# One exp per head with scale, bias and row sum, and one Silu per gate half, in the attention layer of a two-layer trunk

## The chip, the cores and the metric

The kernel runs on one core of one Trainium2 chip. TensorE (PE) multiplies matrices, VectorE (DVE), ScalarE (ACT) and GpSimd (POOL) do the work on elements, and SyncE (SP) issues most of the transfers. The metric is the device time of one execution in microseconds, here the median of several runs.

## The reference

Two layers over 2048 tokens of width 1024. The first is a gated linear recurrence (projection, short convolution, two gates, a scan over time, projection back). The second is an attention layer with 16 query heads of width 64 on 2 key and value heads, a window of 128 tokens, a position term and a learned sink per head. This is the part that matters here:

```python
def sliding_window_sink_attention(q, k, v, sinks):
    ...
    s = jnp.einsum('bnqkgd,bnskd->bnkgqs', qb, kb).astype(jnp.float32) * scale
    ...
    s = jnp.where(valid[None, :, None, None], s + alibi[None, None], -jnp.inf)
    sink = sinks.astype(jnp.float32).reshape(N_KV_HEADS, GROUP)[None, None, :, :, None, None]
    m = jnp.maximum(jnp.max(s, axis=-1, keepdims=True), sink)
    p = jnp.exp(s - m)
    denom = jnp.sum(p, axis=-1, keepdims=True) + jnp.exp(sink - m)
    p = (p / denom).astype(v.dtype)
    o = jnp.einsum('bnkgqs,bnskd->bnqkgd', p, vb)
    return o.reshape(bsz, seq, ATT_WIDTH)

def swa_layer(x, k, v, norm_g, w_in, q_norm_g, sinks, w_out):
    h = rmsnorm(x, norm_g)
    u = h @ w_in
    q, gate = u[..., :ATT_WIDTH], u[..., ATT_WIDTH:]
    q = rmsnorm(q.reshape(bsz, seq, N_Q_HEADS, HEAD_DIM), q_norm_g)
    o = sliding_window_sink_attention(q, k, v, sinks)
    y = o * jax.nn.silu(gate)
    return x + y @ w_out
```

## The kernel before

The kernel has three stages: layer A with channels on the partitions (until about 690 us), the projection out of A by blocks of 128 tokens (until about 955 us), and layer B, the attention layer. Every product of two float32 operands is made of three float16 products (high by high, high by low, low by high), so each value that TensorE is to read is first cut into two float16 parts: a cast and a subtraction.

Layer B works on 16 blocks of 128 tokens. `attend(b)` does the attention of block b; `between(b)` gives the other products that TensorE is to do meanwhile: the key, value and query projections of the next block (`project`), the projection out of the block before (`finish`) and the next block's gate (`project_gate`). `weave` takes so many of these after each step of `attend` as the numbers in `GAPS` say (in ns of TensorE's time). That sets the order in which the program is traced. The framework then orders the instructions of each engine: work that is ready by its own model of times goes first, and among ready work that which was traced first. On the chip each engine takes its instructions in that fixed order.

In `attend`, for each of eight pairs of heads, TensorE makes the scores against the block before and the own block (`o`, 3 buffers in PSUM). ScalarE copies one half to `s` (L961), VectorE puts in the other half by a mask (L962) and adds the position term with the row maximum (L967, one per head). After the fourth pair `soft(0)` works on heads 0 to 7, after the eighth `soft(1)` on heads 8 to 15: VectorE makes the shift `bi` for eight heads at once (L902 to L904), scales and shifts the scores of one head at a time (L906), ScalarE does one Exp over the eight heads (L907) and one for the sinks (L909). `cut` makes the two float16 parts of the weights (L925, L926), `turn` issues the transposing DMA `ppx<-ph` from SP's queue and two masked copies on GpSimd (L933), and `norms` makes the row sums (L913) and their reciprocals. `weigh` multiplies the transposed weights with the values into `po` (TensorE) and takes them out (L949, L950). `pT`, the target of the transpose, has one buffer, so the second half's transpose follows the first half's products. `scale_gate` multiplies the gate by the reciprocal sums on GpSimd (L920), and `gated` multiplies y by it, cuts it and transposes it.

`project` makes the norms of the keys (L810 to L817), their parts (L819), the values (L833 to L843; L842 waits for GpSimd's L841), and the query norms (L854 to L863, with a slow power on GpSimd at L860). `project_gate` makes the gate in two halves of 512 columns: a Sigmoid with a scale from a pointer out of PSUM (L883) and a product on VectorE (L884). The functions Sigmoid and Exp stand in different tables of ScalarE, and an instruction `ACT_TABLE_LOAD` stands ahead of each change from one to the other.

Of the kernel before, what the change touches and what calls it, by code (L numbers as in the profile page):

```python
# [17 lines left out]
AF = mybir.ActivationFunctionType  # L18
# [19 lines left out]
# other products woven in (columns / 2.4) after a block's pair of scores, before the first  # L38
# and the second half of its values; for the first block, the second, those between, the
# last but one, the last  # L40
# [13 lines left out]
def trunk(ctx, tc, x, wA, gw, par, gains, woA, wkv, wB, woB, vec, alib, out):  # L54
# [13 lines left out]
    # ---------------------------------------------------------------- constants  # L68
# [26 lines left out]
    def floor2(mx, n, keep):  # L95
        """[P, n] maxima -> keep [P, n]: each column's maximum over the partitions, rounded
        down to a power of two, on every partition"""
# [21 lines left out]
    # ------------------------------------------------ conv and decay parameters  # L119
# [14 lines left out]
    def decay():  # L134
        # softplus(-lam) = max(-lam, 0) + log1p(exp(-|lam|)), log1p(e) = 2 atanh(e / (2 + e))
# [27 lines left out]
    # ------------------------------------------------------------ shared pieces  # L163
# [3 lines left out]
    def absmax_rows(src, nk, gcol, dest):  # L167
        """largest |gain * w| per partition of src [P, nk, n] -> dest [P, 1]"""
        a = col("amx", nk)
        dve.tensor_reduce(a, src, AX.X, ALU.max, apply_absolute_value=True)  # L170
        dve.tensor_tensor(a, a, gabs[:, gcol : gcol + nk], ALU.mult)
        dve.tensor_reduce(dest, a, AX.X, ALU.max)
# [6 lines left out]
    def split_flat(src, scale, hi, lo):  # L179
        """hi + lo = src * scale in two f16 parts"""  # L180
# [3 lines left out]
    def rstd10(ss, eng):  # L184
        """2**10 / rms of rows of D from their sums of squares"""
# [8 lines left out]
    def normalize(xb, hi, lo, rs=pool):  # L194
        """hi + lo = rows of xb [P tok, D] over their rms, times 2**10"""
# [14 lines left out]
    def flip(src, dest):  # L210
        """dest[:, i, :] = the transpose of src[:, i * P : (i + 1) * P], two-byte types"""
        nc.sync.dma_start_transpose(dest, src)
# [13 lines left out]
    # ======================================================= layer A, channel-major  # L226
# [17 lines left out]
    def xparts():  # L244
        """two [P, D] f16 tiles"""
# [61 lines left out]
    def scales_x(g, W):  # L307
        # |conv(u) + b| <= sum|w| * 2**11 px + max|b|
# [43 lines left out]
    def proj_first(w):  # L352
        """the first chunk's three tiles, token block by token block"""
# [16 lines left out]
    def unit(g, c, W):  # L370
# [36 lines left out]
        def gate(w):  # L407
# [5 lines left out]
            # the fourth block, gathered, on the array's columns 0, 32 and 64  # L413
# [62 lines left out]
    # ---- the first weights and tokens  # L476
# [104 lines left out]
    # ============================================================== out-proj of A  # L581
# [40 lines left out]
    def bstage(n):  # L622
        """[P, n] f32 staging, n <= 2048"""
# [65 lines left out]
    for b in range(NB):  # L689
# [4 lines left out]
        if b == NB - 3:  # L694
            drain(side)
            # the first block of layer B
# [7 lines left out]
    # ======================================================= layer B, token-major  # L704
# [21 lines left out]
    # keys carry g_q * g_k / 8, scaled by a power of two  # L726
# [11 lines left out]
    # slopes halve from head h to head h + 2: queries of head h carry 2**(4 + h // 2), and  # L738
    # two tables do for all heads
# [17 lines left out]
    def eps_of(key, name):  # L757
        # eps in the units of the projection: eps * (2**24 / p)**2
# [12 lines left out]
    # out = P * p_y * (p_wo * p_kv * 2**-31): y carries 2**3 / p_kv, its parts 2**14 / p_y, w_out 2**14 / p_wo  # L771
# [4 lines left out]
    def proj3(o, xt, w, n0, n1, nk=KD):  # L776
        """o[tok, n0:n1] = x @ w in three passes; yields their length after every few products"""
# [23 lines left out]
    def project(b):  # L801
# [4 lines left out]
        # ---- keys  # L806
# [24 lines left out]
        # ---- values: |v| * 2**24 / p < 2**35, kept times 2**-21  # L831
# [13 lines left out]
        # ---- queries  # L845
# [29 lines left out]
    def project_gate(b):  # L875
# [3 lines left out]
        for n in range(2):  # L879
# [3 lines left out]
            act.activation(sl, o, AF.Sigmoid, scale=gscB)  # L883
            dve.scalar_tensor_tensor(sl, o, gscB, sl, ALU.mult, ALU.mult)  # L884
        d["gs"] = gs

    def attend(b):
        """yields how much else the PE is to do, as in GAPS"""
# [271 lines left out]
```

## Time and profile before

| | us |
|---|---|
| median of 3 runs | 1691.45 |
| lowest and highest | 1690.5, 1695.71 |
| span of the profiled execution | 1695.6 |
| TensorE busy | 1550.7 (91%) |
| VectorE busy | 1198.8 (71%) |
| ScalarE busy | 742.7 (44%) |
| GpSimd busy | 475.5 (28%) |

Busy times are sums over the whole span; TensorE's is modelled and overlaps its own weight loads. What a change is worth is read from where TensorE waits, and from what ended last before the wait ended. The granted clock of TensorE is given as a share of full speed.

### The profile page before, as it was taken

To read this page: it belongs to the slowest core of one execution; us is meant where nothing else is said; L and a number is where in the kernel's file an instruction comes from. 1 tells how busy PE (TensorE), PEld (TensorE's weight loads), DVE (VectorE), ACT (ScalarE), POOL (GpSimd) and SP (SyncE) were. 2 spreads that over 40 slices of the span, in tenths; PEclk is the share of its full clock that TensorE was granted. 3 is DMA by queue.
4 is the path that set the end of the run, shared out by engine and by line. 5 is a ranking of instruction groups with operands and counts; after the bars stand their busy time and mean duration, and the time that the engine had idled before them with its cause. 6 is when DMAs were issued, how large, how long until landed. Compare 5 with 4: busy or idle time off the path is not lost.

```text
span 1695.6 us, 23216 instructions
## 1 busy us (share of the span) xinstructions
PE 1550.7 (91%) x8602; PEld 765.2 (45%) x8602; DVE 1198.8 (71%) x2700; ACT 742.7 (44%) x1229; POOL 475.5 (28%) x578
## 2 busy tenths in 40 slices
PE   5988889999999998999799978899999999999986
PEld 4433334444444443444344434455555555555543
DVE  6768878688766677766521269777777777777775
ACT  5656546555445465422200154434444434444332
POOL 2234222211222323000000233524343334334331
PEclk9999999999999999999899989999999999999999
DMA  6563212014311133677731334353344444444322
GB/s 206 142 135 92 79 54 80 24 54 127 106 36 32 57 109 112 220 246 260 283 98 62 117 92 91 78 103 84 85 91 91 91 91 90 88 91 90 66 63 66
DMA packets 242194, 177.29 MB, mean 105 GB/s; under 512 B 204704, under 2 KB 215200, under 8 KB 242080
## 3 DMA queue, kind: packets, MB, share of 16 engines
q1 hardware_dynamic: 233632, 146.95, 33.7%
q0 software_dynamic: 8304, 28.84, 5.0%
q8 instruction: 67, 1.10, 0.3%
q14 instruction: 47, 0.39, 0.1%
q10 hardware_dynamic: 144, 0.01, 0.0%
HBM read 92.93 MB, written 29.36 MB: 72 GB/s over the span
## 4 chain that ended last, share of the span: by engine, by line
PE 35%; DVE 24%; DMA 13%; issue 13%; POOL 7%; ACT 7%; SPq 0%; POOLq 0%; ACTq 0%; DVEq 0%
PE po L117 9%; PE pg L117 9%; PE pu L117 7%; PE pf L117 5%; DMA ppx<-ph 5%; DVE s L906 3%; PE pr L117 3%; DVE s L967 2%; DVE xc L390 2%; POOL hl L393 2%; DVE s L962 2%; DMA x<-x1D 1%; DVE h L448 1%; POOL ppx L933 1%; DMA st<-in_wA_dram 1%
## 5 line engine op out<-in xcount | busy, mean ns | idle before, releaser
L117 PEld LDWEIGHTS <-w 128*128 128x128 f16 x2520 | 238.8, 100 | 274.5 <-issue 22.2
L117 PE MATMUL pu<-xnT,w 128*128 128x512 f16 (+1 forms) x1368 | 262.2, 353 | 3.9 <-ACT ri L423 3.4
L117 PEld LDWEIGHTS <-xT 128*128 128x128 f16 x1920 | 186.9, 98 | 169.8 <-issue 3.8
L117 PE MATMUL pg<-xnT,w 128*128 128x512 f16 x1152 | 259.2, 386 | 0.2 <-DVE w L182 0.2
L117 PE MATMUL po<-wo,xnT 128*128 128x512 f16 x1152 | 252.7, 382 | 1.2 <-ACT ri L423 1.2
L117 PE MATMUL pf<-wob,yT 128*128 128x512 f16 x768 | 186.0, 395 | 3.0 <-DMA yT<-wob 1.9
L117 PE MATMUL pq<-wq,xT 128*128 128x512 f16 x768 | 175.9, 379 | 2.6 <-DVE gs L884 2.6
L117 PEld LDWEIGHTS <-xnT 128*128 128x128 f16 x1152 | 113.0, 98 | 137.5 <-issue 4.9
L117 PE MATMUL pg<-wq,xT 128*128 128x512 f16 x768 | 174.3, 381 | 0.0
L117 PEld LDWEIGHTS <-yT 128*128 128x128 f16 x768 | 74.7, 101 | 88.0 <-issue 7.1
L117 PE MATMUL po<-vt,ppx 128*128 128x128 f16 (+1 forms) x1024 | 65.8, 222 | 49.0 <-DMA ppx<-ph 33.6
L390 DVE SCALAR_TENSOR_TENSOR xc<-u,cwS,xc 128x512 f32<-128x512 f32 x144 | 109.5, 783 | 0.1
L933 POOL TENSOR_SCALAR_AFFINE_SELECT ppx<-ppx 128x1024 f16<-128x1024 f16 x64 | 79.0, 1256 | 65.7 <-DMA ppx<-ph 65.7
L117 PEld LDWEIGHTS <-ppx 128*128 128x128 f16 x1024 | 57.1, 107 | 79.6 <-DMA ppx<-ph 42.1
L385 POOL COPY uhist<-u 128x3 f32<-128x3 f32 x36 | 22.8, 633 | 235.9 <-ACT u L379 235.8
L117 PE MATMUL s<-kT,qT 128*128 128x256 f16 x512 | 75.2, 275 | 12.8 <-DVE s L962 11.7
L950 DVE TENSOR_TENSOR y<-y,po 128x256 f32<-128x256 f32 x64 | 26.7, 417 | 84.9 <-ACT y L949 84.6
L617 DVE SCALAR_TENSOR_TENSOR xnT<-po,cA,xnT 128x512 f32<-128x512 f32 x32 | 23.8, 747 | 88.4 <-PE po L117 88.4
L423 ACT ACTIVATE ri<-pr,pr,rsc 128x512 f32<-128x512 f32 x96 | 67.5, 776 | 42.4 <-PE pr L117 42.3
L906 DVE TENSOR_SCALAR s<-s,ssc,bi 128x128 f32<-128x128 f32 x256 | 84.4, 400 | 0.6
L393 POOL TENSOR_TENSOR hl<-xc,hl 128x512 f16<-128x512 f32 x32 | 58.7, 1842 | 83.9 <-ACT hl L392 83.8
L392 ACT CAST hl<-xc 128x512 f16<-128x512 f32 x48 | 29.6, 617 | 120.1 <-DVE xc L390 113.4
(239 smaller groups left out, 2358.3 us busy)
## 6 DMA issues: line engine op xcount, KB each, us to landing
xnT<-in_wB_dram SPq DMA_DIRECT2D x16, 1024.0 KB, 6.8
yD<-gs POOLq DMA_DIRECT2D x48, 256.0 KB, 2.8
wst<-in_woA_dram SPq DMA_DIRECT2D x24, 512.0 KB, 4.7
xnT<-yD SPq DMA_DIRECT2D x16, 768.0 KB, 6.3
st<-in_wA_dram SPq DMA_DIRECT2D x15, 768.0 KB, 5.4
xs<-in_x_dram SPq DMA_DIRECT2D x16, 512.0 KB, 5.0
xnT<-in_x_dram SPq DMA_DIRECT2D x16, 512.0 KB, 4.4
x1D<-xnT POOLq DMA_DIRECT2D x16, 512.0 KB, 3.3
```

The costliest lines, as they stand in the source:

```text
L117: pe.matmul(o, lhsT, rhs, start=start, stop=stop, skip_group_check=True)
L385: pool.tensor_copy(uhist[:, t], u[:, CH : CH + 3])
L390: dve.scalar_tensor_tensor(xc, u[:, d : d + CH], cw[:, j, d : d + 1], xc, ALU.mult, ALU.add)
L392: act.copy(hl[:, 0], xc)
L393: (pool if j in LO_POOL else dve).tensor_tensor(hl[:, 1], xc, hl[:, 0], ALU.subtract)
L423: act.activation(v, o[j], AF.Sigmoid, bias=pr[:, t, 5 + w : 6 + w], scale=W["rsc"])
L617: dve.scalar_tensor_tensor(xs_, o[n], cA[c], xs_, ALU.mult, ALU.add)
L906: dve.tensor_scalar(s[:, h], s[:, h], ssc[:, h : h + 1], bi[:, h : h + 1], ALU.mult, ALU.add)
L933: pool.affine_select(pU[:, w], pT[:, w], [[0, 8], [-1, P]], ALU.is_gt, 0.0, base=0, channel_multiplier=1)
L950: dve.tensor_tensor(yv, yv, o[:, :, 0], ALU.add)
L962: dve.copy_predicated(sl, mask.unsqueeze(1).to_broadcast([P, 2, P]), o[:, :, 0:P])
L967: dve.tensor_tensor_reduce(s[:, h], s[:, h], al[:, i * P : (i + 1) * P], 1.0, -3.4e38, ALU.add, ALU.max, mr[:, h : h + 1])
```

## The change

In `soft` the scaling on VectorE is gone: ScalarE does one Exp per head, whose scale and bias are taken from columns of `ssc` and `bi`, and which adds up its results along the row into a column of `lsum`. In `norms` the row sum is gone. In `project_gate` the Sigmoid and the product after it are one Silu. The other lines of the diff take out comments and docstrings and are left out here; the lines up to the gate keep their numbers.

```diff
             sl = gs[:, n * CH : n * CH + CH]
-            act.activation(sl, o, AF.Sigmoid, scale=gscB)
-            dve.scalar_tensor_tensor(sl, o, gscB, sl, ALU.mult, ALU.mult)
+            act.activation(sl, o, AF.Silu, scale=gscB)
         d["gs"] = gs
...
             for h in range(8 * n, 8 * n + 8):
-                dve.tensor_scalar(s[:, h], s[:, h], ssc[:, h : h + 1], bi[:, h : h + 1], ALU.mult, ALU.add)
-            act.activation(s[:, hs], s[:, hs], AF.Exp)
+                act.activation(
+                    s[:, h],
+                    s[:, h],
+                    AF.Exp,
+                    bias=bi[:, h : h + 1],
+                    scale=ssc[:, h : h + 1],
+                    accum_out=lsum[:, h : h + 1],
+                )
             dve.tensor_tensor(sk[:, hs], vecs[:, 128 + 8 * n : 136 + 8 * n], bi[:, hs], ALU.add)
             act.activation(sk[:, hs], sk[:, hs], AF.Exp)
 
         def norms(n):
             hs = slice(8 * n, 8 * n + 8)
-            dve.tensor_reduce(lsum[:, hs], s[:, hs], AX.X, ALU.add)
             dve.tensor_tensor(lsum[:, hs], lsum[:, hs], sk[:, hs], ALU.add)
             dve.reciprocal(rl[:, hs], lsum[:, hs])
```

## Rows read from the trace of the kernel before

**Rows 1.** The page's first part: busy us, share of the span, instructions.
```profile
PE 1550.7 (91%) x8602; PEld 765.2 (45%) x8602; DVE 1198.8 (71%) x2700; ACT 742.7 (44%) x1229; POOL 475.5 (28%) x578
```
**Rows 2.** Windows of blocks 5, 6: PE, PEld, DVE, ACT, POOL busy; granted clock; DMA.
```profile
1212.91:1257.10 44.19, 41.73 (x265) 22.78 (x264) 34.56 (x99) 18.86 (x39) 17.42 (x18) 0.96 0.41 87
1257.10:1301.15 44.05, 40.78 (x265) 22.06 (x264) 34.26 (x99) 18.42 (x39) 16.36 (x18) 1.00 0.40 87
```
**Rows 3.** TensorE's waits from 1130 to 1600: waiter, releaser, us, times, longest.
```profile
PE po L117 <- DMA ppx<-ph: 23.4, 11, 2.9
```
**Rows 4.** Windows inside block 5: the wait, and the stretch after it.
```profile
1230.42:1232.87 2.45, 0.00 (x0) 0.00 (x1) 2.35 (x11) 0.24 (x1) 0.00 (x0) 0.99 0.85 159
1232.87:1237.39 4.52, 4.52 (x39) 2.64 (x40) 4.48 (x7) 1.52 (x3) 3.00 (x3) 0.63 0.00 0
```
**Rows 5.** TensorE's waits from 975 to 1130 (blocks 0 to 2).
```profile
PE po L117 <- POOL ppx L933: 7.1, 6, 4.3
PE po L117 <- DMA ppx<-ph: 5.9, 5, 1.9
```
**Rows 6.** TensorE's waits from 1600 to 1695 (the last two blocks).
```profile
PE po L117 <- POOL ppx L933: 5.0, 7, 1.2
...
PE s L117 <- DVE s L962: 1.8, 1, 1.8
```
**Rows 7.** ScalarE's timeline in block 5: start us, us, line, operation, tiles, idle before.
```profile
1217.48 0.22 ACT L810 ACTIVATE kn<-pkv 128x64 f32<-128x64 f32 x1
...
1217.69 0.22 ACT L810 ACTIVATE kn<-pkv 128x64 f32<-128x64 f32 x1
...
1221.69 0.30 ACT L842 CAST vt<-vd 128x128 f16<-128x128 f32 x1 [0.75 <-POOL vd L841]
1221.90 0.64 ACT L961 COPY s<-s 128x256 f32<-128x256 f32 x2
1222.55 1.28 ACT L907 ACT_TABLE_LOAD   x1
1223.85 1.06 ACT L907 ACTIVATE s<-s 128x1024 f32<-128x1024 f32 x1
```
**Rows 8.** VectorE's timeline in block 1 (first row) and block 5.
```profile
1038.16 3.29 DVE L906 TENSOR_SCALAR s<-s,ssc,bi 128x128 f32<-128x128 f32 x5
...
1220.43 0.34 DVE L904 TENSOR_SCALAR bi<-mt 128x8 f32<-128x8 f32 x1
...
1220.89 2.71 DVE L906 TENSOR_SCALAR s<-s,ssc,bi 128x128 f32<-128x128 f32 x8
...
1225.61 0.68 DVE L925 CAST ph<-s 128x1024 f16<-128x1024 f32 x1
...
1227.35 1.21 DVE L926 TENSOR_TENSOR ph<-s,ph 128x1024 f16<-128x1024 f32 x1
```
**Rows 9.** VectorE's groups by line, 975 to 1695: busy us, mean ns, idle before.
```profile
L906 DVE TENSOR_SCALAR s<-s,ssc,bi 128x128 f32<-128x128 f32 x256 | 84.4, 400 | 0.6
...
L913 DVE TENSOR_REDUCE lsum<-s 128x8 f32<-128x1024 f32 x32 | 38.6, 1208 | 0.0
...
L884 DVE SCALAR_TENSOR_TENSOR gs<-pg,gscB,gs 128x512 f32<-128x512 f32 x32 | 23.9, 746 | 3.4 <-ACT gs L883 3.3
```
**Rows 10.** ScalarE's groups by line, whole span.
```profile
L907 ACT ACTIVATE s<-s 128x1024 f32<-128x1024 f32 x32 | 33.8, 1057 | 40.9 <-DVE s L906 40.8
...
L436 ACT ACTIVATE ri<-ri,cneg 128x512 f32<-128x512 f32 x48 | 31.1, 711 | 0.2
...
L438 ACT ACTIVATE q<-q 128x512 f32<-128x512 f32 x48 | 26.7, 619 | 0.2
...
L883 ACT ACT_TABLE_LOAD x17 | 21.8, 1283 | 1.5 <-PE pg L117 1.2
L907 ACT ACT_TABLE_LOAD x17 | 21.8, 1283 | 0.3
```
**Rows 11.** ScalarE's timeline in layer A: three Exps in a row.
```profile
418.99 1.95 ACT L436 ACTIVATE ri<-ri,cneg 128x512 f32<-128x512 f32 x3
```

## The prediction

> **What bounds the kernel now.** I began with the busy times [rows 1]: TensorE is busy for 91% of the span, VectorE (DVE) for 71%. So most of the change, which empties VectorE and fills ScalarE (ACT), happens beside a busy TensorE and can be worth nothing by itself. Only what TensorE waits for counts. Next I cut layer B (the attention layer, the only part that the change touches) into its 16 blocks of 128 tokens. Blocks 3 to 13, eleven of them, are alike, about 44 us each [rows 2]. The view of TensorE's waits over these eleven names one thing: the first product of weights and values (tile `po`) waits for the transposing DMA of the cut weights (`ppx<-ph`), 11 times, 23.4 us in all, or 2.1 us a block [rows 3]. Two windows inside block 5 show what such a wait costs: 2.45 us with no matmul at all, then 4.52 us in which the granted clock is 0.63 of full speed, between its levels of 1.2 and 2.4 GHz. That is 0.37 x 4.52 = 1.7 us more [rows 4]. In block 6 the granted clock is 1.00 over the whole block, although it waits too [rows 2], so the second part is not paid each time. Elsewhere, blocks 0 to 2 lose 13.0 us on `po`, 7.1 for GpSimd's masking of the weights and 5.9 for the DMA [rows 5], and the last two blocks 5.0 us on the masking and 1.8 us on a pair of scores that waits for VectorE [rows 6].
>
> So the question is when the first half of the cut weights is ready. In block 5 the shift `bi` of heads 0 to 7 is done at 1220.77, the eight scalings of line 906 run from 1220.89 to 1223.60, the one Exp starts at 1223.85 and ends at 1224.91, VectorE comes to the cast (L925) at 1225.61, and the subtraction L926 ends at 1228.56, with the row sum L913 (1.21 us) between the two [rows 7, 8]. From `bi` to the end of the cut: 7.8 us. The transpose starts then.
>
> **The change part by part.**
>
> Removed from VectorE: 256 scalings (84.4 us), 32 row sums (38.6 us) and 32 gate products (23.9 us) [rows 9], 147 us in all, 9.2 us a block. VectorE isn't what TensorE waits for as an engine, so only the part in the chain counts. In a steady block that is 2.7 us of scalings, 1.06 us of Exp, 0.7 us of waiting for VectorE's own turn and 1.2 us of row sum.
>
> Added to ScalarE: 256 Exps of 128x128 with a pointer for scale and one for bias, and a read of the accumulator after each, in place of 32 Exps of 1057 ns. No row shows an Exp of this form, so it is bounded from neighbours. An ACTIVATE of 512 elements takes 619 ns without a pointer (L438) and 711 ns with one (L436), so a pointer costs 92 ns; from 512 to 1024 elements it goes from 619 to 1057 ns, 0.855 ns an element [rows 10]. For 128 elements and two pointers: 619 + 2x92 - 384x0.855 = 475 ns. Three in a row take 1.95 us instead of 3x0.711 = 2.13 [rows 11], so each overlaps its neighbour by 0.09 us: a step of 0.385 us. The squares of the keys at L810 are the same kind with an accumulator: the second starts 0.21 us after the first [rows 7], and its own ACTIVATE is 0.22 us [rows 7], so with the 0.09 us of overlap the read adds about 0.08 us. One head: 0.47 us; half a block: 3.75 us and 0.1 us until the last result, 3.85 us in place of 1.06. Bounds: 8x0.385 = 3.1 us if the read hides, and 8x(0.475+0.2) = 5.4 us if nothing overlaps; I take 3.85, since L810 shows the overlap with a read.
>
> ScalarE gains about 8x0.47x2 - 2x1.06 = 5.4 us of work a block. That is covered by its idle time, if it comes at the right moment. What stands behind the Exps on ScalarE are the copies of score pairs 5 to 7 and the evictions of the query projection. VectorE's masking waits for the copies, but the second half's chain has also lost its scalings and its row sum; TensorE has done all eight pairs by then.
>
> A wait that changes place: the Exp no longer waits for L906 but for `bi`. The row of the table load at 1222.55, 1.28 us long [rows 7], lay beside L906 until now and cost nothing. With the scalings gone it stands in the chain. It can't run earlier than the instruction before it on ScalarE, and that is L842, which waits for GpSimd and ends at 1221.99 [rows 7]. From there: load until 1223.3, eight heads until 1227.1, cast and subtraction 1.8 us: 1228.9, against 1228.56 before. Ahead of it, the two gate products no longer delay VectorE, which I put at 0.35 us (an estimate, of the 1.5 us that two of them take [rows 9]; the key norms that come next wait for other engines anyhow). So in a steady block the transpose starts at the same time, within 0.1 us, and the eleven blocks keep their waits: 0 us. Break-even is a first Exp at 1222.9, 2.1 us after `bi`, since 3.85 and 1.8 us follow it.
>
> Whether the copies, L842 or the Exps come first on ScalarE is the choice of the scheduler, which orders ready work by its own model; the trace of before can't show it. With the two copies first, as now, the load starts at 1222.55 as in the row and the cut ends 0.6 us later again; with the Exps ahead of L842, 1.1 us earlier.
>
> The gate: 32 Sigmoids become 32 Silus with the same input; I cost them the same. There are 17 loads before Sigmoids and 17 before Exps [rows 10], about two switches a block, and I keep that number.
>
> The Trainium skill, "ScalarE: Activation LUTs", section "What ACT_TABLE_LOAD costs", puts a switch at 1283 ns and a drain of 1380 ns, 2.66 us together. The trace agrees on the first, and shows no drain: the Exp starts 1.30 us after the load does [rows 7]. If the drain came into the chain as well, the eleven blocks would lose about 15 us and the time would be 1698 us; I give that 0.03, inside the slower rival.
>
> The first blocks: in block 1 five of the scalings take 3.29 us from 1038.16 [rows 8] because y's work and GpSimd's stand between them; the Exps need none of that. There the change can return most of the wait. Of the 13.0 us of blocks 0 to 2 [rows 5] I take two fifths, 5.2 us, as the masking waits in part for GpSimd's own queue; bounds 0 and 9. The last two blocks: the 1.8 us that scores wait for VectorE [rows 6] and part of the 5.0 us, 2.5 us in all; bounds 0 and 4. Sum: -7.7 us, say -8.
>
> Against the profiled execution, whose span is 1695.6 us (0.1 below the slowest of three runs), this gives 1688; the median of the runs is 1691.45, so the forecast is 1683.
>
> **The rivals.**
>
> *Slower: the Exps come late on ScalarE.* The mechanism is the order on ScalarE in the steady block. From the break-even on (first Exp later than 2.1 us after `bi`) every microsecond goes to the start of the transpose and from there to TensorE, eleven times. With the copies ahead it is +0.6 us, with a head at 0.6 us another +1 us: 7 to 18 us on the forecast, and up to 5 us for blocks that would now lose clock as block 5 does: 1690 to 1706 us, middle 1699. Beyond 0.8 us a block the gain of 8 is eaten up and the change is slower than before. For it: ScalarE is in order, and in the row it took both copies before the Exp. Against: the copies went first because the Exp wasn't ready. Chance 0.25. By the Trainium skill, "ScalarE: Activation LUTs", section "Rules for kernel authors", multiplies and adds belong on VectorE rather than ScalarE. Here the trace has a scaling at 0.34 us a head on VectorE and the whole head at an estimated 0.47 us on ScalarE, so that rule would put the time here.
>
> *Faster: the Exps start at once.* If they go ahead of L842, or Silu and Exp need no switch between them, the cut ends 1.0 to 1.6 us earlier. TensorE's wait of 2.1 us shrinks by as much, and blocks that paid 1.7 us of clock as block 5 did get it back in part. 11 x (1.2 + 0.8) = 22 us, with the 8: 1661 us. The floor, with all waits and the clock back, is 11 x 3.8 = 42 us below the forecast. Chance 0.25.
>
> *No change: the gain at the ends doesn't come.* First blocks ruled by loads of weights and GpSimd, steady blocks even: 1691. Chance 0.1.
>
> My forecast, even steady blocks and a gain at both ends, has chance 0.4.
>
> **How the numbers follow.** Likeliest: 1683 us, its own range 1677 to 1690. The range for 8 in 10 takes in the faster rival's middle and most of the slower one: 1658 to 1706. About 0.3%, 5 us, is what a measurement here can tell from no change. Faster by more than that (below 1686.4): 0.26 of the forecast's 0.4, and nearly all of the faster rival, 0.5. Slower (above 1696.5): 0.2, most of the slower rival. Within: 0.3, the rest.
>
> **What would show it.** In the profile after: a pair of Exp and accumulator read at 0.45 to 0.5 us a head; a table load directly ahead of the first Exp of a block, now with VectorE idle beside it; the first Exp 1.5 to 2.5 us after L904; the wait of `po` for `ppx<-ph` in blocks 3 to 13 still about 2 us a block; VectorE's busy time down by some 147 us, ScalarE's up by about 90. The prediction is wrong if the heads cost over 0.6 us each, if the table loads change in number, or if the order of the products on TensorE changes, so that `po` comes at another point between the projections.

## The result, and the profile after

The changed kernel takes 1697.0 us (median of 20 runs, 1694.05 to 1702.45) where the kernel before takes 1690.97 (20 runs, 1683.6 to 1697.36): ratio 1.004, interval [1.003, 1.005]. It is 6 us slower; the forecast was 8 us faster.

The page's first part of the kernel after (compare [rows 1]):

```profile
PE 1550.7 (92%) x8602; PEld 767.2 (45%) x8602; DVE 1056.1 (62%) x2380; ACT 832.1 (49%) x1709; POOL 468.0 (28%) x578
```

VectorE lost 142.7 us, ScalarE got 89.4, and TensorE is as busy as before. ScalarE's groups by line, 975 to 1695 (compare [rows 10]):

```profile
L905 ACT ACTIVATE s<-s,bi,ssc 128x128 f32<-128x128 f32 x256 | 122.8, 481 | 16.9 <-DVE bi L903 16.7
L905 ACT ACTIVATION_READ_ACCUMULATOR s<-s,bi,ssc 128x1 f32 x256 | 47.9, 187 | 0.0
L883 ACT ACT_TABLE_LOAD x17 | 21.8, 1283 | 0.3
L905 ACT ACT_TABLE_LOAD x17 | 21.8, 1283 | 0.3
L883 ACT ACTIVATE gs<-pg,gscB 128x512 f32<-128x512 f32 x32 | 21.8, 681 | 26.1 <-PE pg L117 26.1
```

The Sigmoid of before, whole span:

```profile
L883 ACT ACTIVATE gs<-pg,gscB 128x512 f32<-128x512 f32 x32 | 21.8, 680 | 29.1 <-PE pg L117 29.0
```

The loads are 17 and 17 as before, a Silu takes 681 ns where a Sigmoid took 680. By the Trainium skill, "ScalarE activation tables: per-element evaluation and per-set limits", section "What a function is on this engine", an instruction costs the same whichever function's table it reads; these two rows agree.

TensorE's waits after, first from 975 to 1130 (compare [rows 5]):

```profile
PE s L117 <- DVE s L966: 10.0, 3, 4.4
PE po L117 <- POOL ppx L937: 6.9, 6, 3.5
PE po L117 <- DMA ppx<-ph: 6.3, 4, 2.0
```

The scores had waited as long before:

```profile
PE s L117 <- DVE s L962: 9.9, 4, 5.1
```

From 1130 to 1600 (compare [rows 3]):

```profile
PE po L117 <- DMA ppx<-ph: 24.2, 11, 2.8
```

From 1600 to 1695 (compare [rows 6]):

```profile
PE po L117 <- DMA ppx<-ph: 7.7, 2, 5.7
PE po L117 <- POOL ppx L937: 2.6, 4, 0.9
```

And the wait for the DMA there in the kernel before:

```profile
PE po L117 <- DMA ppx<-ph: 4.4, 1, 4.4
```

In sum the waits did not grow: with the smaller ones they come to 63.9 us in these three stretches, where the two profiles of the kernel before have 66.3 and 69.7. Windows of two steady blocks, and for each its stop ahead of `po` and the 4.5 us behind it (compare [rows 2, 4]):

```profile
1386.10:1430.25 44.15, 41.89 (x265) 23.23 (x264) 24.45 (x79) 23.91 (x69) 16.11 (x18) 0.96 0.46 87
1430.25:1472.96 42.71, 40.44 (x266) 22.09 (x264) 24.45 (x79) 23.78 (x69) 16.66 (x18) 1.00 0.43 90
1404.04:1406.06 2.02, 0.00 (x1) 0.01 (x1) 1.88 (x6) 1.54 (x7) 0.00 (x0) 1.00 0.77 144
1406.06:1410.56 4.50, 4.26 (x39) 2.98 (x40) 2.11 (x6) 3.32 (x13) 4.49 (x3) 0.68 0.00 0
1448.19:1450.17 1.98, 0.00 (x1) 0.01 (x1) 1.84 (x6) 1.51 (x7) 0.00 (x0) 1.00 0.78 146
1450.17:1454.67 4.50, 4.21 (x44) 2.42 (x45) 2.10 (x6) 3.70 (x15) 4.49 (x3) 1.00 0.02 4
```

The two blocks do the same and stop equally long. In the first the granted clock falls behind the stop (mean 0.68 over 4.5 us: partly at 1.2 GHz, partly at 2.4), the block's mean is 0.96, and it is 1.44 us longer. I call a block whose mean is 1.00 a block that keeps the clock. After has 1 such block of the eleven, blocks 3 to 13.

Where the time went, by the starts of the blocks' first scores in TensorE's timeline (us; "before, again" is e22, a second profile):

| | before | before, again | after |
|---|---|---|---|
| start to first scores | 992.5 | 988.4 | 987.8 |
| first scores to block 3 | 130.2 | 129.3 | 131.3 |
| blocks 3 to 13 | 483.5 | 481.3 | 485.7 |
| block 14 to the end | 89.3 | 89.2 | 90.0 |
| mean granted clock of the three stretches from the first scores on | 0.92, 0.97, 0.96 | 0.96, 0.99, 0.95 | 0.91, 0.96, 0.92 |
| of the eleven, blocks that keep the clock | 3 | 8 | 1 |

After loses 1.1 to 2.0 at the start, 2.2 to 4.4 in the eleven blocks and 0.7 or 0.8 at the end: 4.0 to 7.2 us, around the 6 measured. The stretch ahead of the first scores took from 985.4 to 995.2 us over all profiles of this document; in the profile of after it happened to be short, which hides the loss in the spans of the profiles (1694.7 against 1695.6).

A profile shows one execution, but the mean granted clock of every execution is on record. Its median is 0.964 in the 20 runs of after (0.959 to 0.968), and 0.972 in the 100 runs of before made beside the experiments (0.967 to 0.980). One less this clock, times the span, is 61 us in after and 47 in before: 14 us more clock lost, in a kernel that takes 6 us more.

The chain in the steady block that starts at 1386.10, on ScalarE (compare [rows 7]):

```profile
1393.12 0.50 ACT L819 CAST kd<-kn 128x128 f16<-128x128 f32 x2 [0.78 <-DVE kn L817]
...
1393.81 1.28 ACT L905 ACT_TABLE_LOAD   x1
1395.10 0.49 ACT L905 ACTIVATE s<-s,bi,ssc 128x128 f32<-128x128 f32 x1
...
1395.60 0.28 ACT L835 CAST vt<-v 128x128 f16<-128x128 f32 x1
1395.78 0.29 ACT L842 CAST vt<-vd 128x128 f16<-128x128 f32 x1
1395.98 0.49 ACT L905 ACTIVATE s<-s,bi,ssc 128x128 f32<-128x128 f32 x1
...
1398.86 0.48 ACT L905 ACTIVATE s<-s,bi,ssc 128x128 f32<-128x128 f32 x1
```

And on VectorE (compare [rows 8]):

```profile
1391.57 0.22 DVE L812 TENSOR_SCALAR kva<-kss,epsk 128x2 f32<-128x2 f32 x1
...
1393.00 0.16 DVE L903 TENSOR_SCALAR bi<-mt 128x8 f32<-128x8 f32 x1
...
1399.46 0.69 DVE L929 CAST ph<-s 128x1024 f16<-128x1024 f32 x1 [4.95 <-ACT s L905]
...
1400.15 0.44 DVE L966 COPY_PREDICATED s<-mask,s 128x256 f32<-128x256 int32 x1
1400.48 1.22 DVE L930 TENSOR_TENSOR ph<-s,ph 128x1024 f16<-128x1024 f32 x1
```

A head's step is 0.48 us (1395.98 to 1398.86 is six steps). The first Exp comes 1.94 us after `bi`, and the load stands in the chain. But two casts (L835, L842, 0.38 us) stand between heads 0 and 1, and a mask (L966) between cast and subtraction. From `bi` to the end of the cut: 8.54 us (7.5 in before's block at 1388.96), from the first scores to the end of the cut 15.6 (15.0 there). Block 5 of before, from which the prediction worked, was not yet settled: its cut ended 15.64 us after the first scores and its stop was 2.46 us, while blocks 6 to 9 have 15.0 and stops of 1.82 to 2.09.

TensorE's timeline of the same block of after (compare [rows 4], which shows the stop of another block):

```profile
1402.58 1.46 PE L117 MATMUL pf<-wob,yT 128*128 128x512 f16 x6
1406.06 0.23 PE L117 MATMUL po<-vt,ppx 128*128 128x128 f16 x1 [2.02 <-DMA ppx<-ph]
```

And of the kernel before, block at 1388.96:

```profile
1405.43 1.03 PE L117 MATMUL pf<-wob,yT 128*128 128x512 f16 x4
1408.33 0.23 PE L117 MATMUL po<-vt,ppx 128*128 128x128 f16 x1 [1.86 <-DMA ppx<-ph]
```

`po` can start 19.96 us after the block's first scores, in before 19.37. The scheduler now puts six products of `pf` ahead of it, not four, so the stop is only 0.16 us longer than in this block.

### The profile page after: what moved, and what is told of

Same layout as the page of the kernel before. It is cut to its first block, busy times and chain, and to the rows that moved or that the text cites. A ratio compares the mean times of both kernels' runs of the same rounds, so it can differ in the third digit from the quotient of the medians.

```text
span 1694.7 us, 23329 instructions
## 1 busy us (share of the span) xinstructions
PE 1550.7 (92%) x8602; PEld 767.2 (45%) x8602; DVE 1056.1 (62%) x2380; ACT 832.1 (49%) x1709; POOL 468.0 (28%) x578
## 4 chain that ended last, share of the span: by engine, by line
PE 41%; DVE 18%; DMA 13%; ACT 12%; issue 10%; POOL 6%; SPq 0%; POOLq 0%; ACTq 0%; DVEq 0%
PE pg L117 11%; PE po L117 9%; PE pf L117 8%; PE pu L117 7%; DMA ppx<-ph 4%; ACT s L905 3%; PE pr L117 3%; DVE xc L390 2%; POOL hl L393 2%; DMA st<-in_wA_dram 1%; DVE h L448 1%; DMA xnT<-in_wB_dram 1%; DVE s L971 1%; DVE s L966 1%; PE s L117 1%
## 5 line engine op out<-in xcount | busy, mean ns | idle before, releaser
L117 PE MATMUL pf<-wob,yT 128*128 128x512 f16 x768 | 190.2, 400 | 2.0 <-DMA yT<-wob 2.0
L905 ACT ACTIVATE s<-s,bi,ssc 128x128 f32<-128x128 f32 x256 | 122.8, 481 | 16.9 <-DVE bi L903 16.7
L117 PE MATMUL po<-vt,ppx 128*128 128x128 f16 (+1 forms) x1024 | 69.4, 227 | 49.5 <-DMA ppx<-ph 38.2
L117 PEld LDWEIGHTS <-ppx 128*128 128x128 f16 x1024 | 60.8, 110 | 79.3 <-DMA ppx<-ph 46.6
L937 POOL TENSOR_SCALAR_AFFINE_SELECT ppx<-ppx 128x1024 f16<-128x1024 f16 x64 | 75.0, 1194 | 65.7 <-DMA ppx<-ph 65.7
L929 DVE CAST ph<-s 128x1024 f16<-128x1024 f32 x32 | 22.4, 700 | 105.4 <-ACT s L905 105.4
L117 PE MATMUL pr<-hl,gw 128*128 128x512 f16 x288 | 73.2, 396 | 9.5 <-DVE gs L404 6.1
```

The source lines that it names most:

```text
L117: pe.matmul(o, lhsT, rhs, start=start, stop=stop, skip_group_check=True)
L905: act.activation(s[:, h], s[:, h], AF.Exp, bias=bi[:, h : h + 1], scale=ssc[:, h : h + 1], accum_out=lsum[:, h : h + 1],)
L929: dve.tensor_copy(ph[:, 0], s[:, hs])
L937: pool.affine_select(pU[:, w], pT[:, w], [[0, 8], [-1, P]], ALU.is_gt, 0.0, base=0, channel_multiplier=1)
```

## The experiments

Each ratio is to the kernel before on the same chip. "Kept" is the number of the eleven blocks that keep the clock in the one profile of that kernel; "first stop" is TensorE's wait ahead of a steady block's first `po`. The profiled execution is the fastest of its kernel's runs in e5 and e13 and one of the slowest in e9, e18 and e19. So the median granted clock of all runs of a kernel is given at the end, beside the kept blocks. Left out lines of an edit are marked by dots.

### Which part costs

**e1**: the Exp per head and the row sum as in the change; Sigmoid and its product (L884) stay.

> The kernel before with the Exp per head and its row sum alone; the gate keeps Sigmoid and product. Theory A (the chain from the shift `bi` to the transpose of the first half got longer on ScalarE, by the table load and eight heads, in each of the eleven steady blocks): all of the loss is here, ratio to before 1.003 to 1.005, some 1695 to 1699 us. Rival B (the Silu is what costs, by its place in the order of the first blocks or by its own evaluation): ratio 0.998 to 1.001.

Measured: 1684.41 us, 0.9955 [0.9938, 0.9971]. Theory A falls: this part alone is a gain. Kept 8, first stop 1.76 to 1.81. ScalarE's timeline of e1's block at 1421.49:

```profile
1428.15 0.50 ACT L819 CAST kd<-kn 128x128 f16<-128x128 f32 x2 [0.42 <-DVE kn L817]
...
1428.86 0.30 ACT L835 CAST vt<-v 128x128 f16<-128x128 f32 x1
1429.17 1.28 ACT L906 ACT_TABLE_LOAD   x1
1430.47 0.49 ACT L906 ACTIVATE s<-s,bi,ssc 128x128 f32<-128x128 f32 x1
...
1431.15 0.49 ACT L906 ACTIVATE s<-s,bi,ssc 128x128 f32<-128x128 f32 x1
```

Counted from the first scores, load and first Exp come as in after. The key cast comes 0.36 us earlier (6.66, there 7.02), because VectorE takes `kva` (L812) ahead of pair 3's position terms; so L835 fits in ahead of the load, and head 1 comes 0.2 us earlier.

**e2**: the Silu alone.

```diff
-            act.activation(sl, o, AF.Sigmoid, scale=gscB)
-            dve.scalar_tensor_tensor(sl, o, gscB, sl, ALU.mult, ALU.mult)
+            act.activation(sl, o, AF.Silu, scale=gscB)
```

> The kernel before with the Silu alone. Theory A: nothing in the chain of the steady blocks changes, at most two gate products less ahead of the scores on VectorE: ratio 0.998 to 1.000. Rival B: ratio 1.003 to 1.005.

Measured: 1721.19 us, 1.0171 [1.0148, 1.0195], far outside both. ScalarE's waits, 1130 to 1600:

```profile
ACT ppx L197 <- DMA x<-x1D: 27.8, 10, 3.4
```

In e1 that row is 1.0 us. The norm of a coming block waits for the load of its tokens, and scores wait behind it for VectorE (13.2 us); a block takes 45 to 47 us. The same row stands in e3 (25.9) and e6b (27.5). Why this second loop comes up in these three isn't settled; they say little on the question.

**e12**: e1 with `AF.Silu` in place of `AF.Sigmoid` and L884 kept, so that the gate is multiplied by its argument twice and only the time is of use.

> The per-head Exp alone, with Silu in place of Sigmoid and VectorE's multiplication (line 884) left in, so the gate is multiplied by its argument once too often and the output is not the reference's. Every engine's order is word for word that of the Exp alone; only the function of 36 ScalarE instructions differs. T: nothing changes, 1682 to 1687 us (ratio to before 0.994 to 0.998), stop 1.8 us, clock kept in most steady blocks. Rival B (the Silu itself, its table or its time, is what costs the changed kernel its gain): 1694 to 1699 us (1.002 to 1.005).

Measured: 1686.22 us, 0.9971 [0.9956, 0.9986]; kept 7. That is e1's ratio within the two intervals: the Silu as a function costs nothing that these runs can tell, and Rival B falls.

**e9**: the changed kernel with a filler on VectorE.

```diff
             act.activation(sl, o, AF.Silu, scale=gscB)
+            dve.scalar_tensor_tensor(sl, o, 0.0, sl, ALU.mult, ALU.add)
```

> The changed kernel with a filler in place of the multiplication that it removes: VectorE adds 0 times the gate's product to the gate (same tiles, same size, values unchanged). VectorE's work is that of the Exp alone again, but the framework's scheduler still puts the kva instruction behind pair 3's position terms and both vt casts of the ScalarE between heads 0 and 1, as in the changed kernel. T (the order costs, by a chain 0.2 us longer): stop near 2.0 us, clock falls in most steady blocks, 1692 to 1699 us (ratio 1.001 to 1.005). Rival E (the time comes from VectorE being free earlier, for instance through the loop of the next block's norm): as the Exp alone, 1682 to 1688 us (0.994 to 0.998).

Measured: 1695.75 us, 1.0023 [1.0012, 1.0033]; kept 2, first stop 2.00 to 2.02. VectorE has as much to do as in e1 again, but `kva` and the two casts stay where after has them, and the loss stays: it doesn't come from VectorE's lighter load.

### Shorter and longer chains

**e3**: the changed kernel with the table loaded early.

```diff
+        warm = col("warm")
...
+            if hp == 1:
+                act.activation(warm, mr[:, 0:1], AF.Exp, scale=0.0)
             yield gaps[0]
```

> The changed kernel with one more Exp of a single column per block, placed behind the copies of the first two score pairs, so that the switch of the table is made there and not between `bi` and the first head. Theory A: the first Exp starts some 1.3 us earlier after `bi`, the wait of `po` falls from 2.0 to about 0.8 us in blocks 3 to 13, and the time by 11 times 1.2 us and some clock: 1675 to 1686 us, ratio 0.991 to 0.997. Rival B, or a rival C by which the loss sits in the order of blocks 0 to 2: no gain from it, ratio 1.002 to 1.005.

Measured: 1715.51 us, 1.0138 [1.0119, 1.0156]: the norm's loop, as in e2. The load did leave the chain (from `bi` to the end of the cut 7.6 us in place of 8.54), but `bi` comes 8.5 to 9.8 us after the first scores in place of 7.06.

**e4**: the kernel before, row sum queued behind the subtraction.

```diff
-            dve.tensor_reduce(lsum[:, hs], s[:, hs], AX.X, ALU.add)
+            with tc.issue_after(last[0].ins):
+                dve.tensor_reduce(lsum[:, hs], s[:, hs], AX.X, ALU.add)
...
-            dve.tensor_tensor(ph[:, 1], s[:, hs], ph[:, 0], ALU.subtract)
+            last[0] = dve.tensor_tensor(ph[:, 1], s[:, hs], ph[:, 0], ALU.subtract)
```

> The kernel before, unchanged in its work, with the row sum on VectorE queued behind the subtraction of the cut instead of ahead of it. Theory A: 1.1 us less between the Exp and the transpose in each half; in the eleven steady blocks the wait of `po` falls from 2.0 to 0.9 us, and the time by 12 to 20 us, ratio 0.988 to 0.993. If the start of the transpose isn't what TensorE waits for: ratio 0.999 to 1.001.

Measured: 1707.53 us, 1.0092 [1.0076, 1.0109]. The first stop does fall, in most blocks to 1.02 to 1.07, but waits for GpSimd's masked copies take its place. TensorE's waits, 1130 to 1600:

```profile
PE po L117 <- POOL ppx L935: 20.8, 30, 0.8
PE po L117 <- DMA ppx<-ph: 13.4, 11, 1.9
```

Taking the row sum out of the chain gives nothing back: the next one in line is GpSimd. Nine of the eleven blocks keep the clock here, so this kernel loses its time by waiting and not by the clock.

**e5** and **e13**: e1 with one useless copy on ScalarE, in e5 ahead of head 7's Exp, in e13 behind it.

```diff
+                if h == 7:
+                    act.copy(s[:, h], s[:, h])
```

```diff
+                if h == 7:
+                    act.copy(s[:, 0, 0:32], s[:, 0, 0:32])
```

> The first four runs overturned Theory A: the Exp per head alone is a gain (0.9955) and only with the Silu beside it does the kernel lose. New theory T: what decides is the length of TensorE's stop ahead of the first po of a steady block. At 1.8 us (per-head Exp alone) the granted clock stays 1.00 afterwards in 8 of 11 steady blocks; at 2.0 us (the changed kernel) it falls in 10 of 11, and a block in which it falls takes about 1.5 us longer. This kernel is the per-head Exp alone, with one more instruction: the ScalarE copies head 7's scores onto themselves ahead of head 7's Exp (a 128x128 copy in the chain, about 0.2 us; values are unchanged). The order of every other instruction in the steady blocks is that of the Exp alone. T: the stop goes from 1.8 to 2.0 us, the clock falls in most of the eleven blocks, and they take 482 to 487 us in place of 475: 1692 to 1698 us in all (ratio to before 1.000 to 1.004). Rival D (the stop costs only its own length): eleven times 0.2 us, 1685 to 1688 us (0.996 to 0.998).

> In e5 the copy fell into an idle stretch of the ScalarE ahead of the table load, so that the stop ahead of po stayed at 1.8 us and the question stayed open. Here the ScalarE copies 32 columns of head 0 onto themselves behind the eighth head's Exp and ahead of VectorE's cast, in the per-head Exp alone; the other instructions of the steady blocks keep their order on every engine. T (the stop's length decides the clock): the chain and the stop grow by about 0.2 us to 2.0, the clock falls in most of the eleven blocks, these take 482 to 487 us, and the kernel 1692 to 1699 (ratio to before 1.001 to 1.005). Rival D (the stop costs only its own length): eleven times 0.2 us on the 1684 to 1686 of the Exp alone, 1686 to 1689 us (0.997 to 0.999).

Measured: e5 1691.25 us, 0.9997 [0.9982, 1.0012]; e13 1680.09 us, 0.9931 [0.9913, 0.9949]. In e5 the copy ran in idle time ahead of the load, and the stop stayed at 1.76 to 1.84; its profiled run (1682.52 us, kept 9) is 9 us under its own median at the same mean granted clock, 0.972, and no run shows where the slower ones lose their time. In e13 the stop grew by 0.1, not 0.2 (mostly 1.86 to 1.92), and the clock stayed in 7 blocks, so T's stop of 2.0 was not reached. Nor did all else keep its order: behind the first `po` products the scheduler put three products of `pf` ahead of the next 26 `po` where e1 has two. With both, the kernel is no slower than e1.

### The place of kva and of po

**e6b**: the changed kernel, L835 and L842 at lower priority (`tc.high_priority(offset=-60)`), second gap 8500.

> The changed kernel with two edits: the two ScalarE casts of vt, which stand between the first and the second head's Exp, get a lower priority and so come behind the eighth head (0.38 us off the chain), and the second gap of the steady blocks goes from 8000 to 8500, which places po behind eight products of pf in place of six (0.43 us later). T: stop 2.0 less 0.8 is about 1.2 us, clock stays 1.00 in nearly all eleven blocks, a block near 42 us, the eleven 460 to 472 us against 485.7: 1670 to 1684 us (ratio to before 0.987 to 0.996). Rival F (the clock falls after any stop in this place, or the loop is set by another chain such as the norm's transfers): 1690 to 1697 us (0.999 to 1.004).

Measured: 1739.7 us, 1.0289 [1.0267, 1.0311]: the norm's loop again.

**e14** (changed kernel) and **e15** (e1), and **e16** (e1, 10100 in place of 8200):

```diff
-GAPS = ((700, 8000, 9500), (300, 8000, 10500), (700, 8000, 9500), (800, 8000, 12000), (900, 11000, 9500))
+GAPS = ((700, 8000, 9500), (300, 8000, 10500), (700, 8200, 9500), (800, 8000, 12000), (900, 11000, 9500))
```

> The changed kernel with the second gap of the steady blocks at 8200 in place of 8000: po comes behind eight products of pf in place of six, and no other instruction of any engine changes place. T: the stop falls by two products, 0.43 us, from 2.0 to under 1.6 us; the clock stays in 8 or more of the eleven blocks, which take 466 to 476 us in place of 485.7: 1677 to 1688 us (ratio to before 0.992 to 0.998). Rival D: only eleven times 0.43 us come back, 1691 to 1694 us (1.000 to 1.002). Rival F (a later po makes another chain late, such as the next block's norm): over 1697 us.

> The per-head Exp alone with the same gap of 8200: po behind eight products in place of six, everything else in its place. T: the stop falls from 1.8 to under 1.4 us and the clock stays in nearly all eleven blocks: 463 to 471 us for them, 1674 to 1683 us in all (ratio to before 0.989 to 0.995). Rival F: another chain is late, over 1688 us.

> The per-head Exp alone with the second gap at 10100: po behind 16 products of pf in place of six (2.1 us later), so that the first stop should all but vanish; the framework's scheduler also moves the norm's square and split ahead of wob's on ScalarE and xT's transpose ahead of yT's. T and the work alone: eleven blocks of 40.6 to 41.2 us, 447 to 453 us, 1655 to 1668 us in all (0.979 to 0.986). Rival F (the half block behind po, or the norm's transfers, set the end once the stop is gone): 1675 to 1700 us.

Measured: 1702.41 us, 1.0061 [1.0044, 1.0078]; 1702.84 us, 1.006 [1.0041, 1.0079]; 1704.58 us, 1.0079 [1.0062, 1.0097]. Kept 0, 0 and 2. That nothing else moved was wrong: in e14 and e15 the last 16 products of the second half's `po` went behind four of `pg`. The next block's norm comes later (its split on VectorE starts 1.2 us after the first scores in e14, 0.4 in after), the masks with it, and the first stop stays at 2.1 (e14) and 2.0 (e15), with 0.5 for GpSimd behind it. In e16 the first stop is 0.25, and 0.94 and 0.78 for GpSimd follow.

**e20** (changed kernel), **e19** (e1): the same gap, and in `weigh` the second half yields less, so that `po` alone moves.

```diff
-                    yield 800
+                    yield 800 - 300 * n
```

**e17**: the changed kernel with `kva` moved up; **e18**: e17 with e20's edits.

```diff
-        dve.tensor_scalar(kva, kss, 1.0 / HD, epsk, ALU.mult, ALU.add)
+        with tc.high_priority(offset=10):
+            dve.tensor_scalar(kva, kss, 1.0 / HD, epsk, ALU.mult, ALU.add)
```

> The changed kernel with one VectorE instruction moved: kva (the keys' variance) is issued ahead of pair 3's position terms, as in the per-head Exp alone, in place of behind them. ScalarE's and SyncE's orders do not change, po comes behind five products of pf in place of six. Theory T2 (the order costs): kn, the kd casts and the table load come 0.3 us earlier, the eighth head ends near 12.9 us after the block's first scores in place of 13.2, the stop ahead of po is 1.85 to 1.95 us in place of 2.0, the clock stays in six or more of the eleven blocks, these take 473 to 479 us in place of 485.7, and the kernel 1680 to 1690 us (ratio to before 0.994 to 0.999). Rival G (the order is not the cause): as the changed kernel, 1694 to 1699 us (1.002 to 1.005).

> The changed kernel with kva moved up and, in the steady blocks, po behind eight products of pf; the second half's products stay where they are (the wait that the second half's po yields is shortened from 800 to 500 so that they do). T2: stop near 1.3 us, block 41.7 to 42.1 us at the full clock, kept in nine or more of eleven: 460 to 466 us, 1668 to 1680 us in all (ratio to before 0.986 to 0.993). Rival F (something else is late next, such as GpSimd's cut of the transposed weights or the norm): 1684 us or more.

> The per-head Exp alone with po behind eight products of pf in place of six in the steady blocks, and nothing else moved (e15 had also moved the end of the second half's po). T2: stop 1.8 less 0.4 is near 1.4 us, the clock stays in nine or more of the eleven blocks, 42.1 us each: 463 to 469 us, 1674 to 1682 us in all (ratio to before 0.989 to 0.994). Rival F: as e15, over 1690 us.

> The changed kernel with po behind eight products of pf in place of six in the steady blocks, and nothing else moved; kva stays behind pair 3. T2 (the stop's length goes with the clock that is granted behind it): stop 2.0 less 0.43 is near 1.6 us, the clock stays in eight or more of the eleven blocks, 466 to 472 us for them in place of 485.7, 1677 to 1686 us in all (ratio to before 0.991 to 0.997). Rival D (only the stop's own length comes back): eleven times 0.43 us, 1691 to 1693 us (1.000 to 1.001). Rival F: as e14, 1700 us.

Measured: e17 1694.28 us, 1.0013 [0.9997, 1.003], kept 2; e18 1696.46, 1.003 [1.0012, 1.0048], kept 1; e19 1694.13, 1.0005 [0.9987, 1.0023], kept 4; e20 1700.24, 1.0042 [1.0023, 1.0061], kept 0. All four miss. In e18 to e20 the first stop shrank as expected (1.34 to 1.61 in the settled blocks) and a wait of 0.5 to 0.7 us for GpSimd took its place: nothing gained. In e17 the chain did get shorter, `po` starts 19.70 us after the first scores as in e1; but the scheduler, which sees the shorter chain, put only five `pf` ahead of it, so one stop of 2.0 us stayed. Windows of e17: a block, its stop, the 4.5 us behind:

```profile
1385.03:1428.80 43.77, 41.75 (x265) 22.97 (x264) 24.65 (x79) 23.90 (x69) 16.09 (x18) 0.96 0.47 88
1402.75:1404.77 2.02, 0.00 (x0) 0.00 (x1) 1.88 (x6) 1.54 (x7) 0.00 (x0) 1.00 0.77 144
1404.77:1409.27 4.50, 4.50 (x38) 2.79 (x39) 2.09 (x5) 3.25 (x13) 4.48 (x3) 0.62 0.00 0
```

**e21**: e17 with one useless copy of a column behind the eighth head, with which the products of the steady blocks stand in e1's order.

```diff
+                if h == 7:
+                    act.copy(s[:, 0, 0:1], s[:, 0, 0:1])
```

**e22**: the kernel before, profiled again.

> e17 (the changed kernel with kva moved up) with one useless instruction more: the ScalarE copies one column of head 0 onto itself behind the eighth head's Exp. With it the framework's scheduler puts po behind six products of pf, and the order of the TensorE's products in the steady blocks is that of the Exp alone. Theory T3 (what the TensorE does just before po, one long stop or a shorter one, goes with the clock): the chain is longer by at most 0.11 us, the first stop falls from 2.0 to 1.8 to 1.9 us, the clock stays in six or more of the eleven blocks, and the kernel takes 1680 to 1689 us (ratio to before 0.993 to 0.998). Rival H (the place of po is without effect, and e17 loses for another reason, such as VectorE's or ScalarE's order): as e17, 1692 to 1698 us (1.000 to 1.004).

> The kernel before, unchanged, profiled once more. If the number of steady blocks that keep the full clock varies from execution to execution, a profile near the median of 1691 us has five to seven such blocks of eleven in place of three, and its eleven blocks take 476 to 481 us in place of 483.5. If the number belongs to the kernel, it is two to four again, and the 4 us between the profile and the median lie ahead of the first scores.

Measured: e21 1683.93 us, 0.9957 [0.9939, 0.9974], kept 9, as T3 expected. Windows of e21, as for e17:

```profile
1379.87:1422.50 42.63, 40.43 (x265) 22.06 (x264) 24.43 (x79) 23.99 (x70) 16.66 (x18) 1.00 0.46 90
1397.80:1399.71 1.91, 0.00 (x1) 0.00 (x1) 1.81 (x5) 1.55 (x7) 0.00 (x0) 1.00 0.73 139
1399.71:1404.21 4.50, 4.21 (x44) 2.38 (x45) 2.11 (x6) 3.68 (x14) 4.48 (x3) 1.00 0.01 4
```

e21 has the whole change in it, one instruction more on ScalarE than e17, the order of products of e1, and is 10 us faster. e22 (a single run) took 1690.03 us: kept 8, more than either case of the expectation has, but its eleven blocks take 481.3, since blocks 3 to 7 wait longer or in more places; the number of kept blocks varies between executions of one kernel.

## Why the prediction was wrong

The step that failed is "the eleven blocks keep their waits: 0 us". The waits stayed, but the step held the granted clock behind them at what it was, without a reason, and the clock is what the kernel lost. The two gains at the ends, 5.2 and 2.5 us, did not show in the time either.

**Operations: right.** A head's step was put at 0.47 us and is 0.48. The load enters the chain and no drain shows behind it (load 1393.81 to 1395.09, Exp 1395.10); loads stay at 17 and 17, Silu costs what Sigmoid did, the first Exp comes 1.94 us after `bi`, in the 1.5 to 2.5 that was named, below the break-even.

**The chain: mis-sized.** The cut was to end within 0.1 us of before and ends 0.6 later than in the settled blocks, counted from the first scores (in block 5, its example, it ends at the same time, 15.60 against 15.64). Two terms were missing: the casts between heads 0 and 1 (0.38), and the mask between cast and subtraction, with which the two take 2.24 us (1399.46 to 1401.70) in place of 1.8.

**Steady blocks, 0 us: failed by 2.2 to 4.4 us.** The waits are indeed the same, 24.2 us for 23.4 [rows 3]. What the step left out is the clock behind the wait. [Rows 2, 4] showed that a block can keep or lose it; I took the share of blocks that lose it as given. It isn't: it differs from kernel to kernel and from execution to execution. For ten profiles, the median of the first stop, the blocks kept, the time of the eleven blocks, the same less 1.7 us (the 0.37 x 4.52 us of [rows 4]) for each block that lost the clock, and the median granted clock of all runs:

| | ratio | first stop | kept | eleven blocks | less 1.7 each | clock, all runs |
|---|---|---|---|---|---|---|
| before | 1 | 1.96 | 3 | 483.5 | 469.9 | 0.972 |
| before, again | | 1.99 | 8 | 481.3 | 476.2 | 0.977 (one run) |
| after | 1.004 | 2.01 | 1 | 485.7 | 468.7 | 0.964 |
| e9 | 1.0023 | 2.01 | 2 | 484.6 | 469.3 | 0.966 |
| e17 | 1.0013 | 2.00 | 2 | 482.9 | 467.6 | 0.966 |
| e1 | 0.9955 | 1.80 | 8 | 475.4 | 470.3 | 0.972 |
| e5 | 0.9997 | 1.78 | 9 | 472.3 | 468.9 | 0.972 |
| e12 | 0.9971 | 1.79 | 7 | 476.1 | 469.3 | 0.971 |
| e13 | 0.9931 | 1.90 | 7 | 475.2 | 468.4 | 0.972 |
| e21 | 0.9957 | 1.88 | 9 | 473.3 | 469.9 | 0.969 |

As measured the eleven blocks lie up to 13 us apart; without the lost clock nine of the ten profiles agree within 3 us. (The tenth, before again, keeps the clock and waits longer instead.) So in the steady blocks the kernels differ by how many blocks lose the clock. A settled block that loses it takes 43.7 to 44.2 us, 1.0 to 1.6 more than one that keeps it in the same kernel (42.4 to 42.7 where no further wait stands in it). At that rate the 14 us of clock that after loses more cost some 8 to 13 us (an estimate), and the rest of the kernel got 2 to 7 us shorter: the waits did shrink, by 2.4 to 5.8 us over layer B.

What goes with it: in these ten profiles (110 blocks) the clock was kept in 45 of the 55 blocks whose first stop was at most 1.92 us, and in 11 of the 55 with a longer one. That border was chosen with the results at hand, and 32 of the 55 longer stops are those of after, e9 and e17, so the count can't tell the stop from the kernel. Nor is it the whole of it: e18 to e20 lose the clock with 1.34 to 1.61 and a second wait close behind, while 1.8 with 0.27 further on, as in e1, mostly keeps it. No rule of the clock is drawn from this.

That the order of instructions decides, and not the work, is shown by e9 (VectorE's work as in e1, `kva` and the casts placed as in after: loss) and by e17 against e21 (the same work but for one copy; `po` one product later: gain). The order of TensorE's products alone doesn't decide. In the steady blocks it is the same, product by product, in e9 and e13, which lie on the two sides. What differs is that `kva` and a cast of `vt` on ScalarE stand in other places, with what follows from them (e13 also has Sigmoid and the useless copy), and the first stop:

```profile
1364.16 0.23 PE L117 MATMUL po<-vt,ppx 128*128 128x128 f16 x1 [2.00 <-DMA ppx<-ph]
1347.92 0.23 PE L117 MATMUL po<-vt,ppx 128*128 128x128 f16 x1 [1.90 <-DMA ppx<-ph]
```

(The first row is e9's, the second e13's.) That the 0.1 us of stop is itself the cause is argued and not shown. Why the chip drops the clock in one block and not in the next of equal stop stays open.

**First blocks, 5.2 us: failed.** `po` waits 13.2 us in blocks 0 to 2 where it waited 13.0 [rows 5], and all waits of TensorE there come to 26.0 us, in the two profiles of before to 26.6 and 27.0. The scalings in block 1 [rows 8] are gone, and the next in line is late. The chain of waits in after, block 1:

```profile
1039.12 1.13 DVE ph L930
1040.77 1.49 POOL gs L924
...
1045.07 1.40 POOL vd L841
...
1048.23 2.09 POOL ppx L937 x2
```

Seven us of GpSimd's own queue stand ahead of the masked copies; the prediction named that queue and still took two fifths of the wait.

**Last two blocks, 2.5 us: failed.** The wait for GpSimd fell from 5.0 to 2.6 and that of the scores (1.8) is gone [rows 6], but the wait for the DMA rose from 4.4 to 7.7 us. All waits together still fell, from 14.0 (again: 13.4) to 12.3 us. Yet the stretch is 0.7 us longer, for its granted clock is 0.92 in after and 0.96 and 0.95 in before. The last 24 products show it, in before and in after:

```profile
1686.41:1691.76 5.35, 5.34 (x24) 2.27 (x24) 0.75 (x1) 0.00 (x0) 0.00 (x0) 1.00 0.13 49
1683.78:1690.82 7.04, 7.04 (x24) 2.70 (x24) 0.75 (x1) 0.00 (x0) 0.00 (x0) 0.76 0.10 37
```

**The rivals.** "Slower" gave 1699 in the middle, near the 1697 measured, but by luck: its mechanism, a late first Exp, didn't happen. Only its side term, "up to 5 us for blocks that would now lose clock", is what came, and larger. The rule of the Trainium skill, "ScalarE: Activation LUTs", section "Rules for kernel authors", that multiplies and adds belong on VectorE, speaks of such operations by themselves. Folded into an Exp that runs anyway they gain: e1, 0.9955. Listed last among what would make the prediction wrong was a change in the order of the products on TensorE. It came true (`po` behind six products of `pf`, not four), but it isn't what costs: e1, e12 and e21 have those six too and gain.

## What to carry to other kernels

An edit that takes work off an engine also changes what a scheduler with its own model of times does with everything else; compare the instruction orders of the two kernels before any time is explained, and test the order alone by a filler or a moved instruction. Where a stall sits next to a clock that comes and goes, cost it as stall plus the chance of losing the clock, and count kept and lost blocks in more than one profile, or compare the mean granted clock of all runs. The change itself is worth 0.4% once one instruction is moved and one useless copy added (e21); the best kernel run here is e13, 0.9931 of before.

## What the runs showed of the hardware

- Behind stops of about 2 us the granted clock fell in most blocks (10 of 11 in after), to a mean of 0.62 to 0.68 over the next 4.5 us, while a neighbouring block with the same stop kept 1.00. A settled block that lost it took 1.0 to 1.6 us more.
- An Exp with two pointers and accumulator, 128x128: 481 ns and a read of 187 ns, which overlap so that heads follow each other by 0.48 us.
- One ScalarE instruction of 0.2 us put into a queue without gaps makes what follows 0.11 us later (e13).
